# Negated attention scores with a row minimum, and a PSUM bank of its own for the fifth block product

## The chip, the cores and the metric

The kernel runs on one core of a Trainium2 chip. The metric is the device time of one execution in microseconds (us); the time shown is the median of several runs. All waits and durations below come from one profiled execution. TensorE does the matrix products (weight loads are listed apart), VectorE, ScalarE and GpSimd the elementwise work, and SyncE and GpSimd issue the DMA transfers.

## The reference

The reference is one step of a two-layer trunk over 128 context tokens and 512 latent tokens, with 1024 channels. Each layer has a token-mixing sub-layer (windowed grouped-query attention A with a sink logit per head, neighbourhood attention B with a position bias, a Fourier branch C, gates and projections) and a SwiGLU feed-forward layer. Cut to what matters here:

```python
def sink_softmax(s, sink):
    m = jnp.maximum(jnp.max(s, axis=-1, keepdims=True), sink)
    e = jnp.exp(s - m)
    return e / (jnp.sum(e, axis=-1, keepdims=True) + jnp.exp(sink - m))
...
    s_band = jnp.einsum('bnqkgd,bnskd->bnkgqs', qb, kb, preferred_element_type=jnp.float32) * scale
    s_band = jnp.where(valid[None, :, None, None], s_band, NEG_INF)
...
        s_loc = jnp.where(col_ok[None, None, :, :, None, :], s_loc + bias[None], NEG_INF)
...
        p = jax.nn.softmax(jnp.concatenate([s_loc, s_ctx], axis=-1), axis=-1)
...
def swiglu(h, w_ffn_in, w_ffn_out):
    g, u = jnp.split(h @ w_ffn_in, 2, axis=-1)
    return (jax.nn.silu(g) * u) @ w_ffn_out
```

## The kernel before

All 640 tokens are worked on together, channels on the partitions. Every large product is made of three matmuls per 128-row step: weights and activations are split into a high and a low part (ScalarE makes the high part of a weight, `whi` L172, VectorE the low part, `wlo` L173), and high x high, high x low and low x high are added up in PSUM. The program writes the order of the instructions out by hand; each engine works through its own list in that order and waits on semaphores. A planner in Python keeps a virtual time: `step` advances it with each product and slips deferred work, the conditioning layer's sums (`ada_side`, L501 and L503, on VectorE during the feed-forward layer) and the attention's ticks between the products.

**Attention.** One unit is two heads of one block of 128 queries. There are 40 units in a layer (20 of branch A, 20 of B), 80 in all. Each tick moves a new unit one stage on: `att_s` (four matmuls per unit, then for each head L817 on VectorE, which adds the bias or mask to the scores, writes the sum to `P` and keeps the row maximum in `sm`; L819 on GpSimd negates the two maxima), one tick later `att_exp` (two exponentials on ScalarE, L825, with the negated maximum as bias and the row sum as second result; in branch A the sink's share on GpSimd and ScalarE; reciprocal L830 and scaling L832 on VectorE), then `att_tr` (transposes, L842) and `att_av`. The products of the projections and merges stand between the ticks. In `merge`, ScalarE makes a gate (L1342), VectorE multiplies it with a product (L1369), and GpSimd adds it up (L1370); the gate has two buffers. For branch B, `queue_b` fetches the position bias with eight GpSimd DMAs, and GpSimd adds the column mask to it (L1227, six instructions for each of four head pairs in a layer). GpSimd also issues the additions of weight blocks in DRAM (L418).

**Product pairs.** In the feed-forward layer two columns of 128 outputs are made as a pair: seven block products in place of eight, on half the rows and half the tokens each, 12 matmuls a product (L744), 40 pairs in all, with gate pairs and up pairs taking turns. Four PSUM banks are taken from six in turn, one for product 0 (later also 3), one for product 1 (later also 4), one for 2 (later also 5) and one for 6:

```python
        p2 = psum()
        product(1, p2, True, False)
        nc.vector.tensor_tensor(u2, p2, m1, op=OP.add)
        ...
        product(4, p2, False, True)
        nc.vector.tensor_tensor(m1, p2, m1, op=OP.add)
        nc.gpsimd.tensor_tensor(m5, m5, m1, op=OP.subtract)
```

ScalarE copies product 0 to `m1` (L753) and product 2 to `m5` (L761); VectorE adds in L757, L767, L771 and L776. The results go to `evac`: a SiLU on ScalarE for a gate pair (L1543), for an up pair a multiplication on VectorE (L1545), a copy on ScalarE (L1547) and a subtraction on VectorE (L1548).

At the start of a layer's mixing, `mix` issues on GpSimd the DMA of the masks and rotation tables (L972), of the sink logits (L976) and of two blocks of cached keys (L987, L988).

Of the kernel before, what the change touches and what calls it, by code (L numbers as in the profile page):

```python
# [10 lines left out]
F32 = mybir.dt.float32  # L11
# [276 lines left out]
class Kernel:  # L288
# [445 lines left out]
    def pair(self, key, evac):  # L734

        nc, W = self.nc, self.W
        self.tmp = self.tmp[1], self.tmp[0], self.tmp[2]
        m1, u2, m5 = self.tmp

        def product(i, ps, first, last):  # L740
            w, x = W.part(key, i), self.left[i]()
            for k in range(4):
                for j, (p, q) in enumerate(((0, 0), (0, 1), (1, 0))):
                    nc.tensor.matmul(ps, w[p][:, k, :], x[q][:, k, :], start=first and k == 0 and j == 0,  # L744
                                     stop=last and k == 3 and j == 2, skip_group_check=True)

        def end(i):
            W.part_done(key, i)
            self.step(12 * 320 * PE_COL)
        psum = lambda: self.psum("mm")[:, :320]  # L750
        p1 = psum()
        product(0, p1, True, False)
        nc.scalar.activation(m1, p1, AF.Copy)  # L753
        end(0)
        p2 = psum()
        product(1, p2, True, False)
        nc.vector.tensor_tensor(u2, p2, m1, op=OP.add)  # L757
        end(1)
        p3 = psum()
        product(2, p3, True, False)  # L760
        nc.scalar.activation(m5, p3, AF.Copy)  # L761
        end(2)
        product(3, p1, False, True)
        evac(0, p1, 0)
        end(3)
        product(4, p2, False, True)
        nc.vector.tensor_tensor(m1, p2, m1, op=OP.add)  # L767
        nc.gpsimd.tensor_tensor(m5, m5, m1, op=OP.subtract)  # L768
        end(4)
        product(5, p3, False, True)  # L770
        nc.vector.tensor_tensor(u2, p3, u2, op=OP.subtract)  # L771
        evac(1, u2, 0)
        end(5)
        p4 = psum()
        product(6, p4, True, True)
        nc.vector.tensor_tensor(m1, p4, m1, op=OP.add)  # L776
        evac(0, m1, 1)
        evac(1, m5, 1)
        end(6)
# [24 lines left out]
            self.tick()  # L804

    def att_s(self, u):
        nc = self.nc
        n = u["n"]
        P = self.ap.tile([128, 2, 512], F32, name="P", tag="P", bufs=2)
        sm = self.ap.tile([128, 12], F32, name="sm", tag="sm", bufs=4)  # L810
        u["P"], u["sm"] = P, sm
        for h in range(2):
            ps = self.psum("s")[:, :n]
            out = ps if not u["grid"] else ps.rearrange("p (r c) -> p r c", c=32)
            nc.tensor.matmul(out, u["q"][:, h, u["qc"]], u["khi"](h), start=True, stop=False)  # L815
            nc.tensor.matmul(out, u["q"][:, h, u["qc"]], u["klo"](h), start=False, stop=True)  # L816
            nc.vector.tensor_tensor_reduce(out=P[:, h, :n], in0=ps, in1=u["bias"](h), scale=1.0, scalar=u["sink"](h),  # L817
                                           op0=OP.add, op1=OP.max, accum_out=sm[:, h:h + 1])
        nc.gpsimd.tensor_scalar(sm[:, 2:4], sm[:, 0:2], -1.0, None, op0=OP.mult)  # L819

    def att_exp(self, u):
        nc = self.nc
        P, sm, n = u["P"], u["sm"], u["n"]
        for h in range(2):
            nc.scalar.activation(P[:, h, :n], P[:, h, :n], AF.Exp, bias=sm[:, 2 + h:3 + h], accum_out=sm[:, 4 + h:5 + h])  # L825
        if u["sinks"] is not None:
            nc.gpsimd.tensor_tensor(sm[:, 6:8], u["sinks"], sm[:, 2:4], op=OP.add)
            nc.scalar.activation(sm[:, 6:8], sm[:, 6:8], AF.Exp)
            nc.gpsimd.tensor_tensor(sm[:, 4:6], sm[:, 4:6], sm[:, 6:8], op=OP.add)
        nc.vector.reciprocal(sm[:, 8:10], sm[:, 4:6])  # L830
        for h in range(2):
            nc.vector.tensor_scalar(P[:, h, :n], P[:, h, :n], sm[:, 8 + h:9 + h], None, op0=OP.mult)  # L832
# [133 lines left out]
    def mix(self, l):  # L966
# [5 lines left out]
        nc.gpsimd.dma_start(ca[:, :2176], A["c_amask_rope"])  # L972
        self.amask = ca[:, :1152]
        self.rope_t = ca[:, 1152:2176].rearrange("p (a c) -> p a c", a=2)
        self.sink = ap.tile([128, 8], F32, name="sink", tag="sink", bufs=1)
        nc.gpsimd.dma_start(self.sink, self.AP(tensor=A["a_sink"].tensor, offset=A["a_sink"].offset + 8 * l, ap=[[0, 128], [1, 8]]))  # L976

        for i in range(4):
            for g in range(2):
# [113 lines left out]
    def proj_qa(self, p, between=None):  # L1093
# [4 lines left out]
        def ev(ps, g):  # L1098
            if g == 0:
                st["q"] = self.stage()  # L1100
            self.rope_evac(st["q"], 0.125, 128)(ps, g)
        self.proj((self.l, "qa", p), 0, ev)
        if between is not None:
            between()
# [3 lines left out]
    def queue_a(self, p):  # L1108
        kv = p // 2
        q, khi, klo, va = self.qA[p], self.khi, self.klo, self.va  # L1110
        amask, oA = self.amask, self.oA
        sinks = self.sink[:, 2 * p:2 * p + 2]

        spans = (((128, 512), 6, (4, 0, 1)), ((128, 640), 0, (4, 0, 1, 2)), ((384, 896), 1, (1, 2, 3, 4)),
                 ((512, 896), 5, (2, 3, 4)), ((0, 128), 0, (5,)))
# [1 line left out]
        for b, ((k0, k1), m0, vt) in enumerate(spans):  # L1117
# [4 lines left out]
                khi=lambda h, k0=k0, k1=k1: khi[:, kv, k0:k1],  # L1122
                klo=lambda h, k0=k0, k1=k1: klo[:, kv, k0:k1],
                bias=lambda h, m0=m0, n=n: amask[:, 128 * m0:128 * m0 + n],
                sink=lambda h: sinks[:, h:h + 1], sinks=sinks,
                v=lambda i, h, vt=vt: va[:, vt[i], 64 * kv:64 * kv + 64],
                out=oA[:, p, qc]))

# [1 line left out]
    def proj_qb(self, p):  # L1130
# [7 lines left out]
        def evac(ps, g):  # L1138
# [2 lines left out]
            qs = st["q"]  # L1141
            lat = qs[:, 128:640].rearrange("p (n r c) -> p r n c", n=4, r=8)
            if g == 0:
                nc.scalar.activation(qs[:, 0:128], ps[:, 0:128], AF.Copy, scale=0.125)
            src, r0 = (ps[:, 128:384], 0) if g == 0 else (ps, 4)
            sv = src.rearrange("p (r n c) -> p r n c", n=4, c=16)
            for n in range(4):
                if n % 2:
                    nc.vector.tensor_scalar(lat[:, r0:r0 + 4, n, :], sv[:, :, n, :], 0.125, None, op0=OP.mult)
                else:  # L1150
                    nc.scalar.activation(lat[:, r0:r0 + 4, n, :], sv[:, :, n, :], AF.Copy, scale=0.125)
        self.proj2((self.l, "qb", p), evac)
        self.qB[p] = self.stack_q(st["q"])

# [47 lines left out]
    def queue_b(self, p):  # L1202
# [20 lines left out]
        def mask():  # L1223
            for h in range(2):
                for w in range(3):
                    bb = bv[:, 3 * h + w, 0:256].rearrange("p (r c) -> p r c", c=32)
                    nc.gpsimd.tensor_tensor(bb, bb, self.colmask[:, w:w + 1, :].to_broadcast([128, 8, 32]), op=OP.add)  # L1227
        mask()
        self.att_q.extend([None] * BUB_B[p])
        lat = lambda t, h, s: t[:, h, 128:896].rearrange("p (r c) -> p r c", c=64)[:, :, s:s + 32]  # L1230
        for n in range(4):
# [7 lines left out]
                sink=lambda h: -3.0e38, sinks=None,  # L1239
                v=lambda i, h, n=n, rot=rot: v[:, (2 * n + i) if i < 2 else 9 + rot, 64 * h:64 * h + 64],  # L1240
                out=oB[:, p, 128:640].rearrange("p (r n c) -> p n r c", r=8, n=4)[:, n]))
        self.att_q.append(dict(
            key=("B", p), grid=False, n=128, q=q, qc=slice(0, 128),
            khi=lambda h: khi[:, h, 0:128], klo=lambda h: klo[:, h, 0:128],
            bias=lambda h: bv[:, 0, 256:384], sink=lambda h: -3.0e38, sinks=None,
            v=lambda i, h: v[:, 8, 64 * h:64 * h + 64], out=oB[:, p, 0:128]))


# [401 lines left out]
def _constants():  # L1650
# [15 lines left out]
    c["c_dft"] = d.reshape(128, 2048).astype(f)  # L1666
    i = np.arange(128)
    z = np.zeros((128, 128), f)
    prev = np.where(i[None, :] >= i[:, None], 0, NEG).astype(f)
    nxt = np.where(i[None, :] <= i[:, None], 0, NEG).astype(f)  # L1670
# [7 lines left out]
    for w, n in enumerate((0, 1, 3)):  # L1678
# [4 lines left out]
        cm[w] = np.where(ok, 0, NEG)  # L1683
    c["c_colmask"] = np.tile(cm.transpose(1, 0, 2), (8, 1, 1))
    return c

# [58 lines left out]
```

## Time and profile before

| | us |
|---|---|
| median of three runs | 2143.89 (2141.85 to 2143.91) |
| profiled execution: its own time | 2143.28 |
| profiled execution: its span, first to last instruction | 2141.5 |
| TensorE busy with matmuls | 2089.6 (98%) |
| VectorE busy | 1237.4 (58%) |
| ScalarE busy | 912.8 (43%) |
| GpSimd busy | 515.1 (24%) |

A busy time counts the stretches in which an engine has an instruction under way; overlapping matmuls count once. The mean granted clock of TensorE over the span is 0.995 of its upper level.

### The profile page before, as it was taken

What the parts mean: (1) busy time and instruction counts of PE and PEld (TensorE: products, weight loads), DVE (VectorE), ACT (ScalarE), POOL (GpSimd) and SP (SyncE); (2) the same over time, 40 slices, a digit from 0 to 9 for tenths busy, and PEclk for the clock granted to TensorE, in tenths of its full rate; (3) what the DMA queues carried; (4) which work ended last, traced back from release to release, by engine and by line L of the source; (5) the groups of instructions that cost most, each with busy time, mean ns of one, the idle gap of its engine ahead of it and who ended that gap; (6) DMA issues with size and microseconds to landing.
All of it is one profiled execution on the core that took longest, in us unless ns stands there. A gap on an engine that the chain in (4) does not pass through costs nothing.

```text
span 2141.5 us, 35955 instructions
## 1 busy us (share of the span) xinstructions
PE 2089.6 (98%) x13876; PEld 1939.6 (91%) x13876; DVE 1237.4 (58%) x2289; ACT 912.8 (43%) x1947; POOL 515.1 (24%) x783
## 2 busy tenths in 40 slices
PE   6999999999999999999999999999999999999998
PEld 4999999998879889889889999999988798998996
DVE  3555664553357777777466556555533676563663
ACT  3644453432245434235356445434423543541541
POOL 3121325452123100100142124354321320010012
PEclk9999999999999999999999999999999999999999
DMA  8555769894644565554535466798855244442443
GB/s 277 153 115 147 162 194 187 212 212 137 224 157 140 178 186 166 175 162 142 195 110 143 128 150 168 191 195 202 185 177 197 99 141 146 139 148 79 138 153 123
DMA packets 369803, 349.68 MB, mean 163 GB/s; under 512 B 16608, under 2 KB 294144, under 8 KB 369376
## 3 DMA queue, kind: packets, MB, share of 16 engines
q1 hardware_dynamic: 337040, 293.51, 43.8%
q0 software_dynamic: 32160, 53.63, 14.5%
q8 instruction: 109, 1.79, 0.3%
q14 instruction: 62, 0.51, 0.1%
q10 hardware_dynamic: 432, 0.25, 0.0%
HBM read 335.50 MB, written 95.72 MB: 201 GB/s over the span
## 4 chain that ended last, share of the span: by engine, by line
PE 60%; DVE 3%; ACT 2%; POOL 2%; issue 1%; DMA 1%; DVEq 0%; POOLq 0%; ACTq 0%; SPq 0%
PE ps_mm L744 20%; PE ps_mm L650 7%; PE ps_mm L651 7%; PE ps_mm L652 6%; PE ps_mm L1406 5%; PE ps_mm L1408 5%; PE ps_mm L1407 5%; PE ps_t L842 1%; PE ps_o L856 1%; DMA vbt<-in_c_cvb 1%; PE ps_s L815 1%; PE ps_s L816 1%; POOL hT_lo L631 1%; ACT whi L172 1%; DVE wlo L173 0%
## 5 line engine op out<-in xcount | busy, mean ns | idle before, releaser
L173 DVE TENSOR_TENSOR wlo<-wraw,whi 128x512 fp32r<-128x512 f32 (+1 forms) x453 | 408.3, 908 | 406.8 <-ACT whi L172 401.4
L650 PE MATMUL ps_mm<-hT_hi,whi 128*128 128x256 f32 (+2 forms) x1552 | 489.3, 315 | 1.5 <-DVE sg L1369 1.0
L652 PE MATMUL ps_mm<-hT_hi,wlo 128*128 128x256 f32 (+2 forms) x1552 | 480.9, 310 | 0.7 <-DVE wlo L173 0.7
L651 PE MATMUL ps_mm<-hT_lo,whi 128*128 128x256 f32 (+2 forms) x1552 | 480.6, 310 | 0.0
L172 ACT ACTIVATE whi<-wraw 128x512 fp32r<-128x512 f32 (+1 forms) x453 | 354.4, 790 | 287.2 <-PE ps_mm L1408 147.1
L650 PEld LDWEIGHTS ps_mm<-hT_hi,whi 128*128 128x128 f32 x1552 | 292.6, 189 | 11.5 <-issue 7.2
L652 PEld LDWEIGHTS ps_mm<-hT_hi,wlo 128*128 128x128 f32 x1552 | 292.1, 188 | 1.2 <-DVE wlo L173 1.2
L651 PEld LDWEIGHTS ps_mm<-hT_lo,whi 128*128 128x128 f32 x1552 | 292.5, 188 | 0.4
L744 PE MATMUL ps_mm<-S,whi 128*128 128x320 f32 x960 | 212.8, 309 | 5.6 <-DVE tmp L757 5.6
L768 POOL TENSOR_TENSOR tmp<-tmp,tmp 128x320 f32<-128x320 f32 x40 | 53.5, 1336 | 652.3 <-DVE tmp L767 608.7
L744 PE MATMUL ps_mm<-hT_hi,whi 128*128 128x320 f32 x640 | 198.0, 309 | 1.4 <-ACT tmp L753 1.4
L744 PE MATMUL ps_mm<-hT_hi,wlo 128*128 128x320 f32 x640 | 197.3, 308 | 0.0
L744 PE MATMUL ps_mm<-hT_lo,whi 128*128 128x320 f32 x640 | 197.3, 308 | 0.0
L744 PEld LDWEIGHTS ps_mm<-S,whi 128*128 128x128 f32 x960 | 160.1, 188 | 7.1 <-DVE tmp L757 7.1
L1406 PE MATMUL ps_mm<-whi,aT 128*128 128x512 f32 x400 | 158.4, 396 | 0.0
L1408 PE MATMUL ps_mm<-whi,aT 128*128 128x512 f32 x400 | 157.9, 395 | 0.0
L1407 PE MATMUL ps_mm<-wlo,aT 128*128 128x512 f32 x400 | 157.8, 394 | 0.0
L744 PE MATMUL ps_mm<-S,wlo 128*128 128x320 f32 x480 | 148.1, 309 | 0.0
L744 PEld LDWEIGHTS ps_mm<-hT_hi,whi 128*128 128x128 f32 x640 | 120.1, 188 | 3.5 <-ACT tmp L753 2.5
L650 PE MATMUL ps_mm<-o,whi 128*128 128x256 f32 (+1 forms) x384 | 121.1, 315 | 0.0
L744 PEld LDWEIGHTS ps_mm<-hT_lo,whi 128*128 128x128 f32 x640 | 120.2, 188 | 0.2
L744 PEld LDWEIGHTS ps_mm<-hT_hi,wlo 128*128 128x128 f32 x640 | 120.1, 188 | 0.0
(236 smaller groups left out, 3893.8 us busy)
## 6 DMA issues: line engine op xcount, KB each, us to landing
wraw<-in_w_in SPq DMA_DIRECT2D x92, 512.0 KB, 4.3
wraw<-wsum SPq DMA_DIRECT2D x160, 256.0 KB, 3.3
wsum<-in_w_ffn_in POOLq DMA_DIRECT2D x64, 512.0 KB, 7.8
wraw<-in_w_ffn_in SPq DMA_DIRECT2D x120, 256.0 KB, 3.4
wraw<-in_w_ada SPq DMA_DIRECT2D x56, 512.0 KB, 3.8
wraw<-in_w_ffn_out SPq DMA_DIRECT2D x44, 512.0 KB, 4.1
ada_side<-in_w_ada SPq DMA_DIRECT2D x40, 512.0 KB, 3.8
wsum<-in_w_ffn_in SPq DMA_DIRECT2D x32, 512.0 KB, 6.7
```

Of the source, the lines that this page charges most:

```text
L172: self.k.nc.scalar.activation(hi, src, AF.Copy)
L173: self.k.nc.vector.tensor_tensor(lo, src, hi.bitcast(F32), op=OP.subtract)
L631: (lo_on or (nc.gpsimd if q else nc.vector)).tensor_tensor(lo, zq, hi.bitcast(F32), op=OP.subtract)
L650: nc.tensor.matmul(ps, wh, xh[:, c0:c1], start=(k == 0), stop=False)
L651: nc.tensor.matmul(ps, wh, xl[:, c0:c1], start=False, stop=False)
L652: nc.tensor.matmul(ps, wl, xh[:, c0:c1], start=False, stop=(k == K - 1))
L744: nc.tensor.matmul(ps, w[p][:, k, :], x[q][:, k, :], start=first and k == 0 and j == 0, stop=last and k == 3 and j == 2, skip_group_check= ...
L768: nc.gpsimd.tensor_tensor(m5, m5, m1, op=OP.subtract)
L815: nc.tensor.matmul(out, u["q"][:, h, u["qc"]], u["khi"](h), start=True, stop=False)
L1406: nc.tensor.matmul(ps, xh, u.hi[:, i, :], start=st and i == 0, stop=False)
L1407: nc.tensor.matmul(ps, xh, u.lo[:, i, :], start=False, stop=False)
L1408: nc.tensor.matmul(ps, xl, u.hi[:, i, :], start=False, stop=sp and i == 1)
```

## The change

In the pairs, product 4 gets a bank of its own in place of being added to product 1, and L767 adds `u2`, which holds product 0 plus product 1. In the attention the queries are scaled by -0.125, so that the scores come out negated; masks and bias change their sign too, L817 keeps the row minimum (starting from the negated sink), and the exponential takes scale -1 with that minimum as bias. The negation on GpSimd goes; the sink tile holds the sinks and, from one GpSimd instruction per layer, their negatives.

```diff
         p2 = psum()
-        product(1, p2, True, False)
+        product(1, p2, True, True)
         nc.vector.tensor_tensor(u2, p2, m1, op=OP.add)
...
-        product(4, p2, False, True)
-        nc.vector.tensor_tensor(m1, p2, m1, op=OP.add)
+        p5 = psum()
+        product(4, p5, True, True)
+        nc.vector.tensor_tensor(m1, p5, u2, op=OP.add)
         nc.gpsimd.tensor_tensor(m5, m5, m1, op=OP.subtract)
...
             nc.vector.tensor_tensor_reduce(out=P[:, h, :n], in0=ps, in1=u["bias"](h), scale=1.0, scalar=u["sink"](h),
-                                           op0=OP.add, op1=OP.max, accum_out=sm[:, h:h + 1])
-        nc.gpsimd.tensor_scalar(sm[:, 2:4], sm[:, 0:2], -1.0, None, op0=OP.mult)
+                                           op0=OP.add, op1=OP.min, accum_out=sm[:, h:h + 1])
...
-            nc.scalar.activation(P[:, h, :n], P[:, h, :n], AF.Exp, bias=sm[:, 2 + h:3 + h], accum_out=sm[:, 4 + h:5 + h])
+            nc.scalar.activation(P[:, h, :n], P[:, h, :n], AF.Exp, scale=-1.0, bias=sm[:, h:h + 1], accum_out=sm[:, 4 + h:5 + h])
         if u["sinks"] is not None:
-            nc.gpsimd.tensor_tensor(sm[:, 6:8], u["sinks"], sm[:, 2:4], op=OP.add)
+            nc.gpsimd.tensor_tensor(sm[:, 6:8], u["sinks"], sm[:, 0:2], op=OP.add)
...
-        self.sink = ap.tile([128, 8], F32, name="sink", tag="sink", bufs=1)
-        nc.gpsimd.dma_start(self.sink, self.AP(tensor=A["a_sink"].tensor, offset=A["a_sink"].offset + 8 * l, ap=[[0, 128], [1, 8]]))
+        self.sink = ap.tile([128, 16], F32, name="sink", tag="sink", bufs=1)
+        nc.gpsimd.dma_start(self.sink[:, 0:8], self.AP(tensor=A["a_sink"].tensor, offset=A["a_sink"].offset + 8 * l, ap=[[0, 128], [1, 8]]))
+        nc.gpsimd.tensor_scalar(self.sink[:, 8:16], self.sink[:, 0:8], -1.0, None, op0=OP.mult)
...
-            self.rope_evac(st["q"], 0.125, 128)(ps, g)
+            self.rope_evac(st["q"], -0.125, 128)(ps, g)
...
-                    nc.gpsimd.tensor_tensor(bb, bb, self.colmask[:, w:w + 1, :].to_broadcast([128, 8, 32]), op=OP.add)
+                    nc.gpsimd.tensor_tensor(bb, self.colmask[:, w:w + 1, :].to_broadcast([128, 8, 32]), bb, op=OP.subtract)
```

The other lines of the diff turn the sign of the scale in `proj_qb`, of the starting value of the minimum in branch B, and of the constants for both masks.

## Rows read from the trace of the kernel before

**Rows 1.** Page, busy us (share of the span) and instructions.

```profile
PE 2089.6 (98%) x13876; PEld 1939.6 (91%) x13876; DVE 1237.4 (58%) x2289; ACT 912.8 (43%) x1947; POOL 515.1 (24%) x783
```

**Rows 2.** Waits of TensorE: us in total, times, longest.

```profile
PE ps_mm L744 <- DVE tmp L757: 5.6, 6, 1.3
...
PE ps_t L842 <- DVE P L832: 5.0, 3, 2.4
...
PE ps_mm L744 <- ACT tmp L753: 1.4, 3, 0.5
```

**Rows 3.** Timeline, TensorE at the longest wait in the pairs: start, us, instruction [idle before].

```profile
777.24 0.31 PE L744 MATMUL ps_mm<-hT_lo,whi 128*128 128x320 f32 x1
777.39 0.31 PE L744 MATMUL ps_mm<-hT_hi,wlo 128*128 128x320 f32 x1
778.99 0.56 PE L744 MATMUL ps_mm<-S,whi 128*128 128x320 f32 x2 [1.29 <-DVE tmp L757]
779.39 0.31 PE L744 MATMUL ps_mm<-S,wlo 128*128 128x320 f32 x1
```

**Rows 4.** Timeline, VectorE at that wait and in the next pair.

```profile
778.45 0.49 DVE L757 TENSOR_TENSOR tmp<-ps_mm,tmp 128x320 f32<-128x320 f32 x1
...
781.06 0.49 DVE L767 TENSOR_TENSOR tmp<-ps_mm,tmp 128x320 f32<-128x320 f32 x1 [0.32 <-PE ps_mm L744]
...
790.91 0.69 DVE L173 TENSOR_TENSOR wlo<-wraw,whi 128x512 fp32r<-128x512 f32 x1 [0.30 <-ACT whi L172]
...
792.71 0.48 DVE L1545 TENSOR_TENSOR sg<-sg,ps_mm 128x320 f32<-128x320 f32 x1
```

**Rows 5.** Timeline, ScalarE two pairs after that wait.

```profile
802.08 0.42 ACT L753 ACTIVATE tmp<-ps_mm 128x320 f32<-128x320 f32 x1
```

**Rows 6.** Timeline, VectorE ahead of the first long attention wait.

```profile
349.65 0.08 DVE L817 DVE_READ_ACCUMULATOR2_ANT sm<- 128x1 f32 x1
```

**Rows 7.** Timeline, GpSimd ahead of the same wait.

```profile
354.49 1.56 POOL L819 TENSOR_SCALAR sm<-sm 128x2 f32<-128x2 f32 x1
```

**Rows 8.** Timeline, ScalarE ahead of the same wait.

```profile
352.46 0.49 ACT L1342 ACTIVATE sg<-ps_mm 128x384 f32<-128x384 f32 x1 [7.05 <-PE ps_mm L652]
356.09 0.61 ACT L825 ACTIVATE P<-P,sm 128x384 f32<-128x384 f32 x1 [3.13 <-POOL sm L819]
```

**Rows 9.** Timeline, TensorE at the same wait.

```profile
358.10 0.88 PE L842 MATMUL ps_t<-ident,P 128*128 128x128 f32 x6 [2.17 <-DVE P L832]
```

**Rows 10.** Waits of ScalarE: us in total, times, longest.

```profile
ACT P L825 <- POOL sm L819: 16.1, 9, 3.4
```

**Rows 11.** Timeline, ScalarE ahead of the long attention wait of the second layer.

```profile
1412.60 0.49 ACT L1342 ACTIVATE sg<-ps_mm 128x384 f32<-128x384 f32 x1 [7.05 <-PE ps_mm L652]
...
1416.48 0.62 ACT L825 ACTIVATE P<-P,sm 128x384 f32<-128x384 f32 x1 [3.39 <-POOL sm L819]
```

**Rows 12.** Timeline, TensorE at that wait.

```profile
1418.50 1.33 PE L842 MATMUL ps_t<-ident,P 128*128 128x128 f32 x6 [2.43 <-DVE P L832]
```

**Rows 13.** Windows: length, busy of PE, PEld, DVE, ACT, POOL, granted clock, DMA share, GB/s.

```profile
357.00:361.00 4.00, 2.90 (x17) 2.54 (x18) 3.47 (x9) 2.53 (x6) 1.51 (x2) 1.00 1.12 204
...
1418.40:1422.20 3.80, 3.70 (x15) 3.68 (x16) 2.93 (x8) 2.33 (x6) 1.92 (x2) 0.55 1.13 205
```

**Rows 14.** VectorE's groups: count | busy us, mean ns | idle before.

```profile
L817 DVE CUSTOM_DVE_ANT_0 P<-ps_s,bias 128x384 f32<-128x384 f32 x64 | 33.2, 551 | 3.6 <-POOL bias L1227 3.3
```

**Rows 15.** GpSimd's groups: count | busy us, mean ns | idle before.

```profile
L768 POOL TENSOR_TENSOR tmp<-tmp,tmp 128x320 f32<-128x320 f32 x40 | 53.5, 1336 | 652.3 <-DVE tmp L767 608.7 <-ACT whi L172 43.6
L1227 POOL TENSOR_TENSOR bias<-bias,colmask 128x256 f32<-128x256 f32 x48 | 47.1, 1012 | 48.2 <-DMA bias<-in_b_rpbT 48.2
```

**Rows 16.** Source view of L976, the DMA of the sinks.

```profile
DMA to landing us min/median/max: 5.6/5.7/5.7
```

**Rows 17.** Timeline, GpSimd behind the start of the first layer's mixing.

```profile
77.04 0.73 POOL L889 TENSOR_TENSOR rot<-rot,ca 128x256 f32<-128x256 f32 x1 [19.33 <-ACT rot L887]
```

**Rows 18.** Windows, the branch B stretch of layer one: columns as above.

```profile
297.00:490.00 193.00, 189.91 (x1409) 183.74 (x1408) 104.60 (x256) 78.89 (x190) 88.27 (x127) 1.00 0.88 200
```

More of the change, by code (lines that the diff above doesn't have):

```diff
@@ L1111, in queue_a @@
         amask, oA = self.amask, self.oA
-        sinks = self.sink[:, 2 * p:2 * p + 2]
+        sinks, nsink = (self.sink[:, i + 2 * p:i + 2 * p + 2] for i in (0, 8))
         spans = (((128, 512), 6, (4, 0, 1)), ((128, 640), 0, (4, 0, 1, 2)), ((384, 896), 1, (1, 2, 3, 4)),
@@ L1124, in queue_a @@
                 bias=lambda h, m0=m0, n=n: amask[:, 128 * m0:128 * m0 + n],
-                sink=lambda h: sinks[:, h:h + 1], sinks=sinks,
+                sink=lambda h: nsink[:, h:h + 1], sinks=sinks,
                 v=lambda i, h, vt=vt: va[:, vt[i], 64 * kv:64 * kv + 64],
@@ L1143, in evac @@
             if g == 0:
-                nc.scalar.activation(qs[:, 0:128], ps[:, 0:128], AF.Copy, scale=0.125)
+                nc.scalar.activation(qs[:, 0:128], ps[:, 0:128], AF.Copy, scale=-0.125)
             src, r0 = (ps[:, 128:384], 0) if g == 0 else (ps, 4)
@@ L1148, in evac @@
                 if n % 2:
-                    nc.vector.tensor_scalar(lat[:, r0:r0 + 4, n, :], sv[:, :, n, :], 0.125, None, op0=OP.mult)
+                    nc.vector.tensor_scalar(lat[:, r0:r0 + 4, n, :], sv[:, :, n, :], -0.125, None, op0=OP.mult)
                 else:
-                    nc.scalar.activation(lat[:, r0:r0 + 4, n, :], sv[:, :, n, :], AF.Copy, scale=0.125)
+                    nc.scalar.activation(lat[:, r0:r0 + 4, n, :], sv[:, :, n, :], AF.Copy, scale=-0.125)
         self.proj2((self.l, "qb", p), evac)
@@ L1238, in queue_b @@
                 bias=lambda h, var=var: bv[:, 3 * h + var, :],
-                sink=lambda h: -3.0e38, sinks=None,
+                sink=lambda h: 3.0e38, sinks=None,
                 v=lambda i, h, n=n, rot=rot: v[:, (2 * n + i) if i < 2 else 9 + rot, 64 * h:64 * h + 64],
@@ L1244, in queue_b @@
             khi=lambda h: khi[:, h, 0:128], klo=lambda h: klo[:, h, 0:128],
-            bias=lambda h: bv[:, 0, 256:384], sink=lambda h: -3.0e38, sinks=None,
+            bias=lambda h: bv[:, 0, 256:384], sink=lambda h: 3.0e38, sinks=None,
             v=lambda i, h: v[:, 8, 64 * h:64 * h + 64], out=oB[:, p, 0:128]))
@@ L1668, in _constants @@
     z = np.zeros((128, 128), f)
-    prev = np.where(i[None, :] >= i[:, None], 0, NEG).astype(f)
-    nxt = np.where(i[None, :] <= i[:, None], 0, NEG).astype(f)
+    prev = np.where(i[None, :] >= i[:, None], 0, -NEG).astype(f)
+    nxt = np.where(i[None, :] <= i[:, None], 0, -NEG).astype(f)
     mask = np.concatenate([z, prev, z, nxt, z, prev, z, z, nxt], 1)
@@ L1682, in _constants @@
         ok = (k[None, :] >= ws[:, None]) & (k[None, :] < ws[:, None] + 16)
-        cm[w] = np.where(ok, 0, NEG)
+        cm[w] = np.where(ok, 0, -NEG)
     c["c_colmask"] = np.tile(cm.transpose(1, 0, 2), (8, 1, 1))
```

## The prediction

> **What bounds the kernel now.** Four views, in this order. The busy times first: TensorE is busy for 2089.6 of 2141.5 us [rows 1], so a change pays only where it removes a wait of TensorE, or a stretch at its low clock. Then TensorE's waits by releaser [rows 2]. Two of them end at something that this change touches: six waits of 5.6 us in all in the product pairs (L744), ended by the addition L757, and three of 5.0 us at the transposes of the attention (L842), ended by the scaling L832. A third group stands beside the first and is not touched: three waits of 1.4 us on the copy L753. The other waits, at the start and between the layers, end at lines that the diff leaves alone. Third, the timelines of the engines around one wait of each kind. Last, the granted clock behind the two long attention waits.
>
> **What one wait of TensorE costs.** In the pairs, matmuls start 0.15 us apart and last 0.31; the one after 777.39 was due at 777.54 and started at 778.99, 1.45 us late, behind a wait listed as 1.29. The next two took 0.40 us instead of 0.29 [rows 3]. So a wait costs its listed gap and some 0.27 us.
>
> **The fifth bank.** Before, product 4 adds into the bank of product 1, so it waits until VectorE has read that bank in L757. After, it writes a bank of its own; L767 adds u2 (product 0 plus product 1) where it added m1, so it is one operation on as many columns. No instruction is added or removed. The six waits are worth 5.6 + 6 x 0.27 = 7.2 us if all of it stays.
>
> It does not all stay, because VectorE was late, and remains late. At the longest wait VectorE reached L757 at 778.45, and after it had only 0.32 us without work before L767 [rows 4]. TensorE gains 1.56 us there, VectorE's own list 0.32, and another 0.3 to 0.4 at 790.91, where it waited for ScalarE's weight split; 0.7 in all. What comes next is the burst at the end of the following pair, and behind it on ScalarE the copy L753 at 802.08 [rows 5], on which product 3 of the pair after that already waits for almost half a microsecond (1.4 in three waits). That copy moves 0.7 us up, TensorE would be there 1.56 earlier, so this wait grows by some 0.85 and 0.7 us of the 1.56 is kept. The wait on L757 that comes one product later in that pair goes whole: the five shorter waits average (5.6 - 1.29) / 5 = 0.86, with 0.27 they are worth 1.1 each. About 0.1 of this is handed on to the next wait on L753, two pairs later. So these two waits, worth 2.7, give 1.7. The same sequence stands once more in the next part, where I take 1.7 again. Of the other two, one in each layer, the pair behind shows no wait on L753; they give 1.1 each. Sum: 1.7 + 1.7 + 1.1 + 1.1 = 5.6 us. Ends for the range: 3.5 (the copy L753 eats more of it) and 7.2.
>
> The cover of the fifth bank is the order of reuse. Six banks turn; a pair took four and takes five. The tightest reuse is then product 1 of the next pair, in the bank of product 0 of this one, whose last reader in an up-pair is the multiplication at 792.71, done at 793.2 [rows 4]. It is wanted eleven products of 12 matmuls after the one that started at 778.99 [rows 3], 0.15 us apart: at about 798.8. That is 5 us of cover, so nothing is charged.
>
> **The negation on GpSimd goes.** 80 instructions L819. What TensorE lost is at the places where this instruction was late on a busy GpSimd. At the first, VectorE had the row statistic ready at 349.73 [rows 6]; GpSimd, behind six mask additions, DMA issues and two merges, ran L819 at 354.49 for 1.56 us [rows 7]; ScalarE was done with its gate at 352.95 and began the exponential at 356.09, having waited 3.13 for L819 [rows 8]; TensorE waited 2.17 [rows 9]. Afterwards the exponential reads VectorE's result itself and starts at 352.95, where the gate (itself held by GpSimd) ends. That is 3.1 us up against a wait of 2.17: TensorE's wait goes, with 0.9 to spare, and what is late next, the gate's 7.05, ended before it. Worth 2.17 + 0.27 = 2.45. The second wait, the rest of the 5.0 (0.4), gives 0.65; the row of ScalarE's waits for L819 (16.1 us in nine) covers it [rows 10]. In the second layer the gate ends at 1413.09, the exponential waits 3.39 more [rows 11], TensorE 2.43 [rows 12]. And there the clock fell: 0.55 granted over 3.8 us, the lower level of 1.2 GHz [rows 13], which is 3.8 x 0.45 = 1.7 us of lost work. Worth 2.43 + 0.27 + 1.7 = 4.4. Sum for the attention: 7.5 us. Ends: 4.0 (the clock falls all the same, 1.7, and slower masks, below, take 1.8) and 7.5.
>
> The behaviour of the clock is read from those rows: the 2.17 us wait was followed by a granted clock of 1.00, the 2.43 us wait by 0.55. [...]
>
> **What costs nothing, and by what cover.** The sign changes in the query copies, the scale of -1 in the exponential and the constant masks alter operands, not sizes. The minimum in place of the maximum (L817, 160 instructions): no row shows it; it streams the same columns through the same instruction, 551 ns for 384 [rows 14], so I take no change; below that there is nothing to gain, and above it stands twice the time, which is a rival below. The mask becomes a subtraction from a broadcast: GpSimd's subtraction L768 takes 1336 ns for 320 columns and its mask addition 1012 for 256 [rows 15], 4.2 against 4.0 per column, so at most 0.3 us for six masks. If the swapped operands cost 0.3 us each, the masks at the first wait end 1.9 us later, and 1 us of the 2.45 is lost there. The sink tile's negation, one a layer, waits on GpSimd for its DMA, 5.6 us [rows 16]; queued behind it are two loads of cached keys and a small memset. GpSimd's next work comes at 77.04 after 19.33 us without any [rows 17], so they have 13 us to spare. Without that cover it would be 5.7 us a layer.
>
> **The sum.** 5.6 + 7.5 = 13.1 us off the profiled execution's 2143.28 (span 2141.5 and 1.8 around it): 2130.2. The median of the runs shown is 0.6 above that execution, and so I say 2130.5, 0.6% below.
>
> **The rivals.**
> *VectorE keeps the pace of the pairs.* For it: it has only 0.32 us idle behind the longest wait. Against it: it is idle behind the others, and TensorE waits in six of 40 pairs. Then L753 takes back nearly all of the 5.6: 2143.3 - 7.5 = 2135.8.
> *The exponential stays late.* ScalarE's gate waits 7.05 us for GpSimd, and if the merges slip, the start does not move. Then only the pairs gain: 2137.7. Against it: the gate ended 3.13 us before the exponential began.
> *The change does not do what it says:* both together, or new waits of the same size between the layers, where the clock fell in this trace too. Within 4 us of 2143.
> *The banks run out.* A pair that holds five of six banks makes product 1 wait for a reader of the pair before. From 5 us more lateness on VectorE on, each pair would wait for the excess; 0.6 us in each of 40 would be 24, and the time 2130 + 24 = 2154. The Trainium skill (Trainium Kernel Development and Optimization, section Best Practices) says to mind the pressure on PSUM, since regular bubbles can mean that it ran out. The trace does not bear it out: 5 us of cover.
> *Slower: the minimum is a slower instruction.* Its place is L817, twice in each of 80 attention units. At twice its time a unit costs VectorE 1.1 us more (2 x 0.551). VectorE is busy for 104.6 of 193 us in that stage [rows 18], so most would hide; it decides from 0.22 us exposed per unit on (80 x 0.22 = 17.6: the gain and the 0.2% bound). With half of it exposed: 80 x 0.55 = 44 us, less 13: 2174. Nothing in the profile speaks for it except that the instruction is a custom one.
>
> **How the numbers follow.** Chances: the forecast 0.66; VectorE keeps the pace 0.12; the exponential stays late 0.08; no net change 0.08; banks 0.02; slower minimum 0.04. The forecast's own spread is 2126 to 2135: 3.5 to 7.2 from the pairs, 4.0 to 7.5 from the attention, and 1.7 either way for a stretch at low clock between the layers that comes or stays away. The range takes in the next two cases and that stretch twice: 2125 to 2139. What a measurement of this kernel can tell from no change is about 0.2% (4.3 us). Faster: 0.66 + 0.12 + 0.08 = 0.86; same 0.08; slower 0.06.
>
> **What would show it.** Right: no wait of L744 on L757; waits of L744 on L753 grown from 1.4 to between 2 and 4 us; L825 waiting for no GpSimd line; no wait of TensorE on L832 over 1 us; a granted clock of 1.00 throughout the second layer's attention; L817 at 551 ns for 384 columns; the first GpSimd work behind the sink at the same place. Wrong: waits on L753 of 6 us or more, a wait of L744 on L771 or L776 (banks), L817 visibly longer, a wait of the key split on its cached keys, or a fall of the clock in a place that had none.

## The result and the profile after

| | before | after |
|---|---|---|
| median of four runs each, us | 2143.9 (2141.85 to 2144.85) | 2130.56 (2129.11 to 2134.73) |
| ratio, 95% interval | 1 | 0.9944 (0.993 to 0.9958) |
| profiled execution: own time, span | 2143.28, 2141.5 | 2134.73, 2132.9 |

The changed kernel is 0.6% faster, with a median 0.06 us from the forecast. So close an agreement is partly luck: its four executions lie 5.6 us apart, and the profiled one is the slowest of them. The pages are therefore compared stretch by stretch.

First the busy times, which answer to [rows 1], and then TensorE's waits of after, which answer to [rows 2] (total, times, longest).

```profile
PE 2084.2 (98%) x13876; PEld 1937.1 (91%) x13876; DVE 1240.0 (58%) x2289; ACT 911.0 (43%) x1947; POOL 495.2 (23%) x705
```

```profile
PE ps_mm L744 <- ACT tmp L753: 2.3, 3, 1.1
PE ps_mm L652 <- DVE wlo L173: 1.5, 3, 0.6
PE ps_s L817 <- DVE sm L819: 1.4, 1, 1.4
...
PE ps_t L843 <- DVE P L833: 0.3, 1, 0.3
```

The 5.6 us on L757 are gone. The waits on the copy L753 grew from 1.4 to 2.3. The transposes (L842 before, L843 now) wait 0.3 where they waited 5.0. The row on `wlo` (L652) grew too; its waits stand at the start and in the merge of layer two. In the attention one row is larger than before: 1.4 us at the score matmuls (L817 now), which wait until VectorE's score instruction (L819 now) has read their PSUM buffer.

At the place of [rows 8] and [rows 11], ScalarE starts the exponential (L826 now) right behind the gate, in both layers.

```profile
354.43 0.49 ACT L1344 ACTIVATE sg<-ps_mm 128x384 f32<-128x384 f32 x1 [7.04 <-PE ps_mm L652]
354.82 0.61 ACT L826 ACTIVATE P<-P,sm 128x384 f32<-128x384 f32 x1
...
1406.87 0.49 ACT L1344 ACTIVATE sg<-ps_mm 128x384 f32<-128x384 f32 x1 [7.04 <-PE ps_mm L652]
1407.26 0.61 ACT L826 ACTIVATE P<-P,sm 128x384 f32<-128x384 f32 x1
```

The granted clock is 1.00, its upper level of 2.4 GHz, over the whole attention stretch of layer two. The windows around both places (columns as in [rows 13]) show TensorE busy throughout, at the same level:

```profile
340.00:361.00 21.00, 21.00 (x146) 20.96 (x145) 13.48 (x23) 9.02 (x19) 14.00 (x14) 1.00 0.70 132
1405.00:1421.00 16.00, 16.00 (x111) 15.75 (x111) 10.43 (x27) 7.35 (x19) 12.24 (x15) 1.00 1.06 197
```

The edits charged at nothing or little, in the groups of VectorE and of GpSimd, and the source view of the sink's negation:

```profile
L819 DVE CUSTOM_DVE_ANT_0 P<-ps_s,bias 128x384 f32<-128x384 f32 x64 | 33.1, 550 | 3.2 <-POOL bias L1229 2.9
```

```profile
L1229 POOL TENSOR_TENSOR bias<-colmask,bias 128x256 f32<-128x256 f32 x48 | 47.6, 1022 | 48.8 <-DMA bias<-in_b_rpbT 48.8
```

```profile
  DMA sink<-in_a_sink: 9.6, 2
```

The minimum takes 550 ns where the maximum took 551 [rows 14]. The mask as a subtraction takes 1022 where the addition took 1012 [rows 15]. The negation of the sinks waits for its DMA, 4.8 us per layer. Behind it GpSimd still has 14.31 us without work:

```profile
79.08 0.74 POOL L890 TENSOR_TENSOR rot<-rot,ca 128x256 f32<-128x256 f32 x1 [14.31 <-ACT rot L888]
```

**Where the time went.** The spans are cut at waits of TensorE that stand in both traces. The first two rows of the table run from the wait on `uT` to the last attention unit's wait on `PT` (57.78 to 489.95 us before). The third and fourth run from the end of the feed-forward layer's first waits on `hT_lo` to the wait on `y` behind it in layer one (658.09 to 1091.71) and to the end in layer two.

| us | before | after | difference | forecast |
|---|---|---|---|---|
| attention, layer 1 | 432.17 | 429.85 | -2.3 | -3.1 |
| attention, layer 2 | 435.32 | 431.27 | -4.1 | -4.4 |
| feed-forward, layer 1 | 433.62 | 428.53 | -5.1 | -4.5 |
| feed-forward, layer 2 | 428.70 | 428.03 | -0.7 | -1.1 |
| start, to 57.78 before | 57.78 | 59.82 | +2.0 | 0 |
| merge of layer 2 | 129.28 | 130.79 | +1.5 | 0 |

The four stretches that the change reaches give 12.1 us of the forecast 13.1. The last two rows, at which the diff does not aim, take 3.5 back in this execution. The third experiment tells whether these belong to the change.

### The profile page after: what moved, and what is told of

Same layout as the page of the kernel before. It is cut to its first block, busy times and chain, and to the rows that moved or that the text cites. A ratio compares the mean times of both kernels' runs of the same rounds, so it can differ in the third digit from the quotient of the medians.

```text
span 2132.9 us, 35929 instructions
## 1 busy us (share of the span) xinstructions
PE 2084.2 (98%) x13876; PEld 1937.1 (91%) x13876; DVE 1240.0 (58%) x2289; ACT 911.0 (43%) x1947; POOL 495.2 (23%) x705
## 4 chain that ended last, share of the span: by engine, by line
PE 63%; DVE 3%; ACT 2%; issue 1%; POOL 1%; DMA 0%; DVEq 0%; POOLq 0%; ACTq 0%
PE ps_mm L744 22%; PE ps_mm L650 7%; PE ps_mm L651 7%; PE ps_mm L652 7%; PE ps_mm L1408 5%; PE ps_mm L1410 5%; PE ps_mm L1409 5%; PE ps_o L857 1%; PE ps_t L843 1%; PE ps_s L817 1%; PE ps_s L818 1%; POOL hT_lo L631 1%; DVE wlo L173 0%; ACT whi L172 0%; DMA wraw<-in_w_branch 0%
## 5 line engine op out<-in xcount | busy, mean ns | idle before, releaser
L652 PE MATMUL ps_mm<-hT_hi,wlo 128*128 128x256 f32 (+2 forms) x1552 | 481.6, 310 | 1.5 <-DVE wlo L173 1.5
L652 PEld LDWEIGHTS ps_mm<-hT_hi,wlo 128*128 128x128 f32 x1552 | 292.3, 188 | 2.4 <-DVE wlo L173 2.4
L651 PEld LDWEIGHTS ps_mm<-hT_lo,whi 128*128 128x128 f32 x1552 | 292.7, 189 | 0.5
L1372 POOL TENSOR_TENSOR m<-m,sg 128x384 f32<-128x384 f32 x64 | 65.1, 1040 | 311.2 <-DVE sg L1371 299.5
L1344 ACT ACTIVATE sg<-ps_mm 128x384 f32<-128x384 f32 x96 | 41.6, 435 | 189.5 <-PE ps_mm L652 186.6
```

Source lines behind the costliest of these rows:

```text
L651: nc.tensor.matmul(ps, wh, xl[:, c0:c1], start=False, stop=False)
L652: nc.tensor.matmul(ps, wl, xh[:, c0:c1], start=False, stop=(k == K - 1))
L1344: lambda ps, g: self.nc.scalar.activation(sg[:, GROUPS[g][0]:GROUPS[g][1]], ps, AF.Tanh, scale=0.5))
L1372: nc.gpsimd.tensor_tensor(m, m, s, op=OP.add)
```

## The experiments

Each kernel was timed in turns with the kernel before, whose medians there were 2143.1 to 2144.0. Ratios are to that kernel. "Stretch" means one of the table above.

**1 and 2. Each part alone.** The kernel before with only the fifth bank, and with only the lines of the scores.

```diff
-        product(4, p2, False, True)
-        nc.vector.tensor_tensor(m1, p2, m1, op=OP.add)
+        p5 = psum()
+        product(4, p5, True, True)
+        nc.vector.tensor_tensor(m1, p5, u2, op=OP.add)
```

> The kernel before with the fifth bank alone. My theory, two separate mechanisms: about 2138.5 us (5.6 below before), no wait of L744 on L757, waits of L744 on L753 between 2 and 3 us, the attention's long waits on L832 (2.2 and 2.4 us) as before. Rival, VectorE sets the pace of the pairs: within 2 us of before, with the waits on L753 grown to 5 us or more. Rival, the two parts need each other: less than half of 5.6.

> The kernel before with the negated scores alone. My theory: about 2136.5 us (7.5 below before), six waits of L744 on L757 of 5.6 us as before, no wait over 0.5 us on L832, and the new wait of 1.4 us at the scores of the first layer (on L819), which is in the trace of the changed kernel, again. Rival, the attention is worth little and the bank made the gain: above 2141. Rival, the new wait of 1.4 us is chance: it is not there.

The bank alone took 2135.09 us, ratio 0.9965 (0.9953 to 0.9978); the scores alone 2135.17, ratio 0.996 (0.9947 to 0.9974). TensorE's waits with the bank alone:

```profile
PE ps_t L843 <- DVE P L833: 4.5, 3, 2.2
...
PE ps_mm L744 <- ACT tmp L753: 2.4, 3, 1.1
...
PE ps_s L816 <- DVE sm L818: 0.8, 1, 0.8
```

and with the scores alone:

```profile
PE ps_mm L744 <- DVE tmp L757: 5.5, 6, 1.3
...
PE ps_mm L744 <- ACT tmp L753: 1.7, 4, 0.5
...
PE ps_s L816 <- DVE sm L818: 1.3, 2, 1.1
```

Both came out below what was expected, the bank by 3.4 us and the scores by 1.3. The trace of the bank alone is of its slowest execution, 2141.47 us, and does not show what made the other four (2134.71 to 2136.37) faster.

Each part removes its own waits and leaves the other's. The bank shortens the feed-forward of layer one from 433.62 to 428.76; the scores leave it at 433.18. The scores shorten the two attention stretches to 429.44 and 431.46; the bank leaves them at 432.63 and 435.17. So the parts act in different places. Their ratios together (0.0035 + 0.004 = 0.0075) are not told apart from that of the changed kernel (0.0056, and 0.0068 in the same turns). Whether the gains add up exactly stays open. The wait at the scores stands in both traces, also in that of the bank alone, whose attention is the one of before; experiments 9 and 10 take it up.

**3. The changed kernel once more,** to see what of its trace repeats.

> The changed kernel once more, as the measure for the others on the same chip: 2129 to 2133 us. If the waits of 1.4 us at the scores (first layer) and of 1.0 us at the last merges (second layer) come from the changed order of the GpSimd queue, both are in this profile too; if they come from chance in the transfers, at least one is missing.

It took 2129.93 us, ratio 0.9932 (0.992 to 0.9944). Its start ends at 57.75, and its merge of layer two takes 129.27 without the 1.0 us of waits there: the 3.5 us lost in both in the first execution are not the change's. The waits on L753 (2.4) and the wait at the scores repeat, the latter with 1.59 us at 406.6. So that wait is not one execution's alone.

**4. Products 3 and 4 swapped.** The forecast was that the waits on L753 grow because TensorE comes to product 3 sooner than ScalarE has copied product 0. In the swapped kernel product 4, which needs no copied bank, stands in between.

```diff
-        product(3, p1, False, True)
-        evac(0, p1, 0)
-        end(3)
         p5 = psum()
         product(4, p5, True, True)
...
         end(4)
+        product(3, p1, False, True)
+        evac(0, p1, 0)
+        end(3)
```

> The changed kernel with products 3 and 4 in the other order, so that product 0's copy L753 has one product (1.76 us) more before product 3 adds into its bank. If the rest of the pairs' gain was handed to the wait on L753, that wait (2.3 us listed in three, some 3.6 us by the distances of the products) goes to under 0.5 and the time falls by about 3.5 us, to 2127. If VectorE itself sets the pace, the wait moves on to another product (L761, L771 or a weight split) and the time stays within 1 us of the changed kernel.

It took 2128.27 us, ratio 0.9927 (0.9915 to 0.994). The row of its waits:

```profile
PE ps_mm L744 <- ACT tmp L753: 0.6, 1, 0.6
```

The wait goes from 2.3 to 0.6 (under 0.5 was expected) and the feed-forward of layer one from 428.53 to 426.54, 2.0 us less. Most of what L753 took back from the fifth bank is thus recovered by one more product of time for the copy. The median is 1.7 us below that of the changed kernel in the same turns, where 3.5 were expected, and the intervals overlap.

**5 and 6. The instruction, or its lateness?** Two kernels separate the negation from its place in GpSimd's queue. One is the changed kernel with the 80 old negations kept on GpSimd, their result read by nobody. The other is the kernel before with the negation on VectorE, right behind the instruction that makes its input.

```diff
+        nc.gpsimd.tensor_scalar(sm[:, 2:4], sm[:, 0:2], -1.0, None, op0=OP.mult)
```

> The changed kernel with the old GpSimd negation still issued after each unit, its result read by nobody. Theory, the new wait of TensorE at the scores (1.1 to 1.6 us near 406) comes from GpSimd running ahead without that instruction, so that its weight additions fill the DMA queue and the next position bias and its masks come later and run beside VectorE's key split: the masks start some 3 us earlier than in the changed kernel and the wait falls to 0.8 us or less, while the long attention waits on the scaling stay away; time within 1.5 us of the changed kernel. Rival, the wait comes from TensorE's being earlier alone: it stays at 1.1 us or more.

```diff
-        nc.gpsimd.tensor_scalar(sm[:, 2:4], sm[:, 0:2], -1.0, None, op0=OP.mult)
+        nc.vector.tensor_scalar(sm[:, 2:4], sm[:, 0:2], -1.0, None, op0=OP.mult)
```

> The kernel before with the negation moved from GpSimd to VectorE, nothing else. Theory, what TensorE lost was GpSimd's lateness and not the instruction: the two long waits on L832 (2.2 and 2.4 us) are gone although the 80 negations are still made, the waits on L757 stay, and the time is that of the negated scores alone, 2135 to 2137. Rival, the negation as a step of the chain costs time wherever it runs, or VectorE is too full for 80 more instructions: above 2140.

The first took 2129.71 us, ratio 0.9933 (0.992 to 0.9945), which is the changed kernel's time: the instructions as such cost nothing that can be measured. Its wait at the scores is still 1.10 us at 405, so GpSimd's lighter queue is not what makes that wait; the theory that it is falls. The second took 2138.75, ratio 0.9973 (0.9961 to 0.9984), some 2 us above what was expected; its trace (span 2136.7) has 6.0 us less in the attention and 0.9 more at the start than that of before. ScalarE in it, at the place of [rows 8]:

```profile
353.45 0.49 ACT L1342 ACTIVATE sg<-ps_mm 128x384 f32<-128x384 f32 x1 [7.06 <-PE ps_mm L652]
353.84 0.61 ACT L825 ACTIVATE P<-P,sm 128x384 f32<-128x384 f32 x1
```

The exponential follows the gate with all 80 negations still made, and its attention stretches take 429.72 and 431.79 us, near the 429.85 and 431.27 of the changed kernel. What cost the time was GpSimd's queue ahead of the negation. The 2 us beyond the expected time go with the clock. The mean granted clock of this kernel's executions is 0.995 or 0.996, but for the fastest, 2134.23 us at 0.999; with the scores alone it is 0.996 to 0.999. This trace has 0.66 granted in 1096 to 1101 and in 1707 to 1712 us, that of the scores alone 1.00 from 1090 to 1100 and from 1700 to 1712. No run shows why the one kernel met more such stretches than the other.

**7 and 8. Without VectorE's other work in the feed-forward.** The forecast put the pairs' waits down to VectorE being late. Here the kernel before and the changed one run without the accumulations L503, seven of the eight parts of each conditioning sum.

```diff
                     if k == 0:
                         nc.vector.tensor_scalar(acc[:, s, :], u.raw, c, None, op0=OP.mult)
-                    else:
-                        nc.vector.scalar_tensor_tensor(acc[:, s, :], u.raw, c, acc[:, s, :], op0=OP.mult, op1=OP.add)
```

> The kernel before without the accumulating instructions of the conditioning sums on VectorE in the feed-forward layers (L503 left out, so that each modulation value is made from one of eight parts of its sum). Theory, VectorE is late at L757 because of these sums: the waits of L744 on L757 (5.6 us) fall to under 1, and those on L753 to under 1, and the time is 8 to 12 us below before. Rival, the pairs' own burst on VectorE makes it late: the waits on L757 stay over 3 us.

> The changed kernel without the same accumulating instructions (L503 left out in the same way). Theory: the waits on L753 (2.3 us) fall to under 1; the fifth bank then has nothing left to remove, so that this kernel and the kernel before without the sums differ by the attention's part alone, 6 to 9 us. Rival, the bank is worth its 5 us in any case: they differ by 11 us or more.

The kernel before takes 2131.6 us so, 12.4 less where 8 to 12 were expected (ratio 0.9942, 0.9927 to 0.9958), the changed one 2125.23 (0.9914, 0.99 to 0.9927). In the first, no wait of the pairs on the addition or on the copy is left; in the second, one of 0.3 us on the copy. The 6.4 us between the two are the attention's part: in their traces the two attention stretches differ by 6.1 us (433.41 to 429.48 and 433.63 to 431.42), the two feed-forward stretches together by 0.5. So the bank is worth something here only because the sums make VectorE late. VectorE in the changed kernel, ahead of the addition at which the longest wait stood [rows 4], shows them, three of 1.2 us in one block:

```profile
773.00 3.67 DVE L503 SCALAR_TENSOR_TENSOR ada_side<-ada_side,ada_st 128x1024 f32<-128x1024 f32 x3
776.59 0.68 DVE L173 TENSOR_TENSOR wlo<-wraw,whi 128x512 fp32r<-128x512 f32 x1
777.19 0.48 DVE L757 TENSOR_TENSOR tmp<-ps_mm,tmp 128x320 f32<-128x320 f32 x1
```

**9 and 10. The new wait at the scores.** In the kernel before, GpSimd's masks were done when VectorE was half through its split of the keys (`klo`, `khi`). First VectorE, then GpSimd, in the kernel before:

```profile
398.31 1.09 DVE L1211 TENSOR_TENSOR klo<-stage,khi 64x896 fp32r<-64x896 f32 x1 [0.56 <-ACT khi L1210]
399.41 1.07 DVE L1213 CAST khi<-stage 64x896 fp32r<-64x896 f32 x1
400.51 1.09 DVE L1211 TENSOR_TENSOR klo<-stage,khi 64x896 fp32r<-64x896 f32 x1
401.61 0.62 DVE L1213 CAST khi<-stage 64x896 fp32r<-64x896 f32 x1
```

```profile
394.09 5.91 POOL L1227 TENSOR_TENSOR bias<-bias,colmask 128x256 f32<-128x256 f32 x6 [6.18 <-DMA bias<-in_b_rpbT]
```

Counted from the start of their stretches (57.78 and 59.82), the split starts 2.7 us earlier in the changed kernel, and the masks, held by their DMA, 1.3 later (in its second trace they start where they did before, and the split again 2.7 earlier). VectorE, GpSimd, and TensorE's wait behind them:

```profile
397.64 1.44 DVE L1213 TENSOR_TENSOR klo<-stage,khi 64x896 fp32r<-64x896 f32 x1 [0.56 <-ACT khi L1212]
399.09 1.07 DVE L1215 CAST khi<-stage 64x896 fp32r<-64x896 f32 x1
400.19 1.52 DVE L1213 TENSOR_TENSOR klo<-stage,khi 64x896 fp32r<-64x896 f32 x1
401.73 1.08 DVE L1215 CAST khi<-stage 64x896 fp32r<-64x896 f32 x1
```

```profile
397.40 6.70 POOL L1229 TENSOR_TENSOR bias<-colmask,bias 128x256 f32<-128x256 f32 x6 [7.86 <-DMA bias<-in_b_rpbT]
```

```profile
408.53 0.45 PE L817 MATMUL ps_s<-khi,qst 128*128 128x384 f32 x1 [1.45 <-DVE sm L819]
```

Now all four instructions of the split run beside the masks and take 5.11 us (1.44 + 1.07 + 1.52 + 1.08) in place of 3.87. Counted in the same way, VectorE's score instruction (407.36 before, 407.91 now) comes 1.5 us earlier and TensorE 2.7 us, and the 1.2 between them are the growth of the wait, 0.23 to 1.45.

The same place in the other traces shows what sets the wait (the split is the sum of its four instructions):

| trace | split, us | TensorE's wait, us |
|---|---|---|
| before without the sums | 3.41 | none |
| before | 3.87 | 0.23 |
| bank alone | 4.46 | 0.82 |
| changed without the sums | 4.73 | 1.08 |
| scores alone | 4.74 | 1.08 |
| negation kept | 4.76 | 1.10 |
| products 3 and 4 swapped | 4.76 | 1.11 |
| negation on VectorE | 4.91 | 1.26 |
| changed | 5.11 | 1.45 |
| changed, second trace | 5.24 | 1.59 |

Wherever there is a wait, it is the split's time less 3.65 us, within 0.01, in kernels whose split and whose TensorE come early and in those where they don't. So TensorE's being earlier makes no wait by itself; the slower split does. The wait is not all the change's either: in the first three traces this attention is that of before, and the wait is 0 to 0.82, as the masks end earlier or later against the split. In the other seven the split starts 2.1 to 4.3 us earlier than in those three, all or nearly all of it beside the masks, and the wait is 0.9 us longer on the mean (1.24 against 0.35).

Two kernels test this, both with products 3 and 4 swapped as well. One has no masks in branch B, the other has the second copy of the keys on ScalarE.

```diff
-        mask()
```

> Left out of the changed kernel with products 3 and 4 swapped: the six subtractions of the column mask from the position bias on GpSimd in branch B (the scores there are not masked), nothing else. Theory: the wait of TensorE at about 405 us on the scores' PSUM buffer (1.11 us in the swapped kernel, 1.45 in the changed one) comes because GpSimd's masks (6.68 us from 393.37) now run at the same time as VectorE's split of the keys, which is slower beside them: 1.11 + 1.07 + 1.51 + 1.07 = 4.76 us where the same four took 1.09 + 1.07 + 1.09 + 0.62 = 3.87 before the change. Then without masks the four take about 2 x 1.09 + 2 x 0.62 = 3.4 us, VectorE's score instruction starts 1.3 us earlier and the wait of 1.11 goes or falls to under 0.2; the time is about 1 us less than that of the swapped kernel, 2127. Rival: VectorE is behind there whatever GpSimd does, because TensorE is 3 us earlier; then the wait stays at 0.8 or more.

```diff
-            nc.vector.tensor_copy(khi[b, h, :], ks[a, :896])
+            nc.scalar.activation(khi[b, h, :], ks[a, :896], AF.Copy)
```

> The changed kernel with products 3 and 4 swapped and, in the split of the keys of branch B, the second copy of the keys on ScalarE in place of VectorE. Theory: this takes 2 x 1.07 us off VectorE's list ahead of the score instruction at 404.6 and puts 2 x 0.96 us on ScalarE, which was without work for 3.6 us there; the wait of 1.11 us at about 405 goes, and the time is about 1 us less than that of the swapped kernel: 2127. Rival: ScalarE is late next (its query copies, weight splits and gates stand behind the two copies, in each of 8 head pairs), and a wait of 1 us or more on a ScalarE line comes in its place at this or another head pair: 2128 to 2132.

VectorE without the masks:

```profile
395.27 1.08 DVE L1213 TENSOR_TENSOR klo<-stage,khi 64x896 fp32r<-64x896 f32 x1 [0.56 <-ACT khi L1212]
396.37 0.62 DVE L1215 CAST khi<-stage 64x896 fp32r<-64x896 f32 x1
397.02 1.09 DVE L1213 TENSOR_TENSOR klo<-stage,khi 64x896 fp32r<-64x896 f32 x1
398.12 0.62 DVE L1215 CAST khi<-stage 64x896 fp32r<-64x896 f32 x1
```

and with the copies moved to ScalarE:

```profile
394.66 1.51 DVE L1213 TENSOR_TENSOR klo<-stage,khi 64x896 fp32r<-64x896 f32 x1 [0.56 <-ACT khi L1212]
396.60 1.12 DVE L1213 TENSOR_TENSOR klo<-stage,khi 64x896 fp32r<-64x896 f32 x1 [0.43 <-ACT khi L1212]
```

Without masks the split takes 3.41 us and TensorE has no wait at the scores; the attention of layer one takes 427.97 us against 429.32 in the swapped kernel. With the copies on ScalarE the wait is gone as well, and that stretch takes 427.78. ScalarE, the rival, does not become late: TensorE's waits in the attention hold no new row. The times are 2124.44 us, ratio 0.9914 (0.9901 to 0.9928), and 2124.88, ratio 0.9919 (0.9905 to 0.9932). Both came out 2 to 3 us under the expected 2127. Of that the second layer's attention explains 0.4 and 0.7 (431.51 swapped; 431.10 and 430.77), and the rest isn't told apart from the spread, the intervals overlapping that of the swapped kernel. The kernel before was 0.75 us faster in these turns too (2143.14 against 2143.89); by the ratios, the two lie 2.8 and 1.7 us below the swapped kernel. The trace with the copies on ScalarE is of its fastest execution: its feed-forward stretches take 424.32 and 426.16 us against 426.54 and 427.85, with 1.00 granted from 652 to 662 and from 1693 to 1703, where the swapped kernel's trace has 0.66 from 654 to 659 and from 1698 to 1703. What is shown is the wait's going. The kernel with the swap and with the copies on ScalarE leaves nothing of the reference out, and has the lowest median of those that leave nothing out.

## Why the prediction was right

**The fifth bank: right in mechanism, 5.6 us forecast, 6.2 measured in the pairs.** Taken from start to start of the products, the six pairs that waited and the three with a wait on L753 lost 1.09 us (the pair at 701), 2.02 (769 to 833), 2.02 (928 to 966) and 1.10 (1748) between before and after; forecast were 1.1, 1.7, 1.7 and 1.1. The wait on L753 that the text singled out grew from 0.42 to 1.05, by 0.63 and not 0.85:

```profile
800.34 0.42 PE L744 MATMUL ps_mm<-hT_hi,whi 128*128 128x320 f32 x1 [1.05 <-ACT tmp L753]
```

```profile
799.87 0.42 ACT L753 ACTIVATE tmp<-ps_mm 128x320 f32<-128x320 f32 x1
```

The copy itself, 802.08 before [rows 5], moved up 1.99 us against the start of its stretch, of which 1.09 is the earlier pair's gain; the 0.90 that are left stand against a forecast of 0.7. The other wait of that kind grew by 0.33. So VectorE handed on less of its lateness than the text had it. No pair waited for a bank. Over the whole stretches 5.8 us are seen; the 0.4 that lack stand in layer two. About 0.24 of it lies ahead of the first pair there (18.86 us from the cut to the pair at 1731.66 before, 19.10 to the pair at 1723.97 after), where both traces have a stretch at the low clock (0.72 granted from 1710 to 1716 us before, 0.66 from 1704.5 to 1709.5 after); in the second trace of the changed kernel, which has none there, that way takes 17.56.

**The attention: 7.5 forecast, 6.4 measured (5.7 in the second trace of the changed kernel).** The waits of 2.17, 0.4 and 2.43 us went as the text said, and by its cause: GpSimd's lateness. One reading was wrong: the gate's 7.05 us are not held by GpSimd. Its row names TensorE's product, whose last matmul ends at 352.37, just ahead of the gate at 352.46, and in the changed kernel the gate waits 7.04 all the same.

```profile
352.03 0.34 PE L652 MATMUL ps_mm<-hT_hi,wlo 128*128 128x384 f32 x1
```

The forecast doesn't need that reading; the rival in which the exponential stays late rested on it. The step that was mis-sized is "what is late next". The text looked only as far as the gate. What became late next stands 50 us further on, at the scores: a wait of 1.45 us (0.23 before), since VectorE came to the next head pair's keys earlier against the masks of GpSimd. With that the first layer gave 2.3 and not 3.1. The text had said that TensorE's other waits stand at the start and between the layers and end at lines that the diff leaves alone. The view of before has one in the attention that doesn't, and it is the one that grew:

```profile
PE ps_s L815 <- DVE sm L817: 0.2, 1, 0.2
```

**The clock: a fall costs about what the text says, but its tie to the wait is not borne out.** In the kernel before without the sums, whose two long attention waits are 2.18 and 2.09 us, the first was followed by the low level and the second was not (windows of 4 us, columns as in [rows 13]):

```profile
357.00:361.00 4.00, 3.84 (x15) 3.70 (x16) 3.02 (x9) 2.47 (x6) 1.93 (x2) 0.59 1.13 206
1410.00:1414.00 4.00, 3.87 (x23) 3.51 (x24) 3.02 (x9) 2.44 (x6) 1.93 (x2) 1.00 1.13 205
```

In the kernel before it was the other way round [rows 13]. The attention stretch of layer two takes 433.63 us without the sums and 435.32 in the kernel before: 1.7 us, the size that the text had worked out, but 0.34 of that is the shorter wait, which leaves some 1.4 for the clock. In layer one the stretch with the fall takes 433.41 and that of the kernel before 432.17, 1.2 more. With the bank alone the fall came in layer two again, behind a wait of 2.18 us and not behind one of 1.68:

```profile
358.00:362.00 4.00, 3.15 (x18) 2.79 (x19) 3.47 (x9) 2.53 (x8) 1.76 (x2) 1.00 1.12 205
1415.20:1419.20 4.00, 3.81 (x15) 3.76 (x16) 3.02 (x8) 2.50 (x6) 1.92 (x2) 0.58 1.13 206
```

Over the three kernels that keep these waits (before, the bank alone, before without the sums), three of six were followed by a fall. The Trainium skill (TensorE: Matmul & The Clock Gate, HAM oscillation) tells of falls behind waits that are longer than these; that a wait of about 2 us is followed by one in some traces and not in others is shown here alone. So the term of 4.4 us was 2.7 and a chance of 1.2 to 1.7; the profiled execution of the kernel before happened to have it.

**What was charged at nothing cost nothing.** The minimum, the masks, the sink's negation and the order of the banks behaved as the text said, and the rivals fell: the waits on L753 stayed at 2.3 (6 or more was the mark of the first rival), the exponential wasn't late, both parts acted, no bank ran out, and L819 kept its 550 ns. One of the text's signs of being wrong did come: between the layers the clock fell right behind the wait on `y` (0.66 granted from 1087 to 1092 us), where the kernel before had 1.00 (1092 to 1097) and fell behind that (0.66 from 1097 to 1102). In both traces it is one stretch there.

**The sum.** 12.1 us in the four stretches, against 13.1: the pairs gave 0.2 more than forecast over whole stretches, the attention 1.1 less. That the median fits to 0.06 us is then chance of the size of a stretch at low clock. The working has slips as well: 2130.2 and the 0.6 above the profiled execution make 2130.8 and not 2130.5; the terms of the spread give about 2127 to 2138 and not 2126 to 2135; and the lower end of the attention takes 1.8 us for slower masks, where the text's own working has 1 us lost.

## What to carry to other kernels

When a wait of the bounding engine is removed, look one work item further on each engine that now comes earlier: what had been done just before it arrives (here the masks on GpSimd) now runs beside it, and a part of the gain is given back there. A single tiny instruction on an engine with a long queue is dear by its place, not by its size: moving it next to the instruction that makes its input did in the attention what removing it did. Where a copy frees a buffer, putting a product that doesn't need that buffer in between adds no instruction, and here took 1.7 of 2.3 us of wait away.

## What the runs showed of the hardware that was not expected

VectorE's instructions on 64 x 896 elements take longer while GpSimd's masks run: the copy 1.07 us beside them and 0.62 alone, the subtraction 1.08 to 1.68 beside them (1.68 with the bank alone) and 1.09 alone. With the masks left out all four fall to 1.09 and 0.62. The Trainium skill (GPSIMD Engine Reference, Specifications) says that GpSimd shares its memory interfaces with VectorE and names instructions with two inputs from that memory, and a mode with two ports. The subtraction has two such inputs, and the trace agrees in part: some of the subtractions beside the masks are not slower. In which mode the copy runs, no run here shows. The price, 0.45 us for a copy and none to 0.6 for a subtraction, is from these rows.

The granted clock fell to its lower level behind waits of about 2 us in some executions and not in others, at the same place of the same kernel: the changed kernel's first trace has 0.66 granted in the window from 1704.5 to 1709.5 us, behind a wait of 1.85; its second has the same wait and 1.00 in the windows from 1700 to 1707, and that stretch takes 426.71 us against 428.03.
